# A single ring of up-projected expert inputs, 30 tiles deep, in a fused pooling/retention/PEER block on one core

## Chip, core and metric

One NeuronCore of a Trainium2 chip runs the whole block in one launch. The metric is device time in microseconds (us); three runs of the kernel before took 1885.77, 1891.47 and 1893.0, median 1891.47. The profiled execution is another run of the same kernel.

## What is computed

The input is 512 latent tokens and 256 context tokens of width 1024, all in float32. A first half (adaptive norm, pooling mixer, bidirectional retention, gated merge) ends in a residual x. The change lies in the second half, a product-key expert layer with 128 x 128 = 16384 single-neuron experts:

```python
q = (hb @ wq).reshape(t, 8, 2, 128)
s = einsum('thpd,hpkd->thpk', q, keys)
s1, i1 = top_k(s[:, :, 0], 16); s2, i2 = top_k(s[:, :, 1], 16)
cand = s1[..., :, None] + s2[..., None, :]      # 16 x 16 pairs per head
best, pos = top_k(cand, 16)                     # 16 experts per token and head
g = softmax(best)
act = gelu(einsum('thkd,td->thk', u[eidx], hb))
y = einsum('thk,thkd->td', g * act, v[eidx])
```

Then x + g2 * y goes through a final RMSNorm.

## The kernel before

Matrix products are made in three parts (`mm3`, lines 155 to 157): each float32 operand is split into a rounded high part (`hi`, a cast on ScalarE, line 167) and a low part (`lo = raw - hi`, line 172, on VectorE or GpSimd), and hi*hi, lo*hi and hi*lo are added up in PSUM. Weight tiles arrive as 128 x 1024 float32 (512 KB) in a ring of NRAW = 3 raw buffers, all by DMAs on SP's queue; hi and lo have four buffers each.

Of the 512 tokens the last 384 (NB = 3 blocks of 128) are computed *densely*: all 16384 experts are evaluated, and a matrix G of routing weights (zero where an expert was not chosen) masks them. The first block of 128 tokens is *gathered*: its 128 chosen experts per token are fetched one at a time by indirect DMA (a fetch is 128 rows of u and v, 1 MB).

The expert part runs under a manual schedule: each engine executes in the order in which the program issues, and a wait holds up all that is behind it on the same engine or DMA queue. Its stages:

1. **Queries** (`heads`, 735 to 862). For eight heads: load and split `wq`, project, score against the keys, and run the top-k of the dense blocks (`topk`, a generator: `next` advances it by one step: best 16 of each half, pair sums and index sums on GpSimd, best 16 of 54 pairs with one-hots `oh`, product `oe`, reduction to expert numbers `ef`). Between them run the first *ups*.
2. **An up** (`up_steps`, 1068): for expert column tile j, 24 matmuls give hT x u[j] (128 experts x 384 tokens) in PSUM, and a Gelu on ScalarE writes tile `a` of 384 columns (line 1077). `ups` (864) makes the first AHEAD = 24 of them ahead of the loop; `run_up(n)` advances it by n halves of an up. The tiles lie in `a0`, a block of 22 that shares a pool with the first block's top-k, and in a ring of NA = 3.
3. **Routes** (994): softmax, expert numbers split into two 7-bit halves, everything turned by transposes and copied wide to fp16 (`i12`, `gq`).
4. **One-hots and weights** (1023 to 1056, loop at 1140): in 24 steps of 16 tokens VectorE makes one-hots (`eq`, `o1`, two products `o2`), TensorE multiplies them into the block of G, ScalarE evicts it (`st`) and writes it to DRAM (`gd`); half an up runs in each step.
5. **The dense loop** (1166 to 1220), 128 rounds. Round j adds `a[j]*G[j]` times v[j] into six PSUM banks Y (`down`, 18 matmuls), makes `ph` and `pl` for round j+1, splits v for the next round, splits u and runs the up of tile j + LA (so the first 21 rounds have none, and the lead of 24 is used up by them down to LA = 3). G is read back in 16 pages of 8 tiles (`place`, 1086). In rounds below VU = 19 v is split by GpSimd, else by VectorE. `tick` (1129) advances the first block's top-k, a new head every second round. From round GATHER = 21 on, 1.5 experts per round (CREDIT) are fetched, multiplied (`dot`, 960) and added (`combine`, 969), both on VectorE, two rounds after they were asked for. NUV = 6 fetch buffers are taken from the space that `a0` and the top-k leave.
6. **The tail** (1221 on): the last Y matmuls, final norm and output.

Of the kernel before, what the change touches and what calls it, by code (L numbers as in the profile page):

```python
# [39 lines left out]
AHEAD = 24  # L40
NA = 3
A0 = AHEAD - NA + 1
LA = 3
VU = 19
END = 125
LATE = 114
GATHER = 21
LAG = 2
CREDIT = 1.5
# [89 lines left out]
class Build:  # L139
# [67 lines left out]
    def build(self):  # L207
        nc, tc, I = self.nc, self.tc, self.I
        with ExitStack() as es:
            dr = es.enter_context(tc.tile_pool(name="dram", bufs=1, space=bass.MemoryType.DRAM))  # L210
# [482 lines left out]
    def peer(self):  # L693
# [6 lines left out]
        self.ioh = mr.tile([P, P], F16, name="ioh")  # L700
        self.early = ExitStack()
        self.queries()

    def queries(self):
        nc, tc, I = self.nc, self.tc, self.I
        hT = self.hT
        with tc.tile_pool(name="out", bufs=1) as p:
# [7 lines left out]
        self.a0 = self.early.enter_context(tc.tile_pool(name="a0", bufs=1, side="right")).tile(  # L715
            [P, A0, NB * P], F32, name="a0")
# [6 lines left out]
        self.iota = tp.tile([P, P], F32, name="iota")  # L723
        nc.sync.dma_start(self.iota, I["kc"][:, K_IOTA:K_IOTA + P])
        nc.gpsimd.tensor_copy(self.ioh, self.iota)
        s0 = tp.tile([P, PH, 1, 2, P], F32, name="s0")
        self.acts, self.us = [], {}
        with tc.manual_schedule():
            self.heads(kp, s0, h0)
            es.close()  # L730
            self.topk0 = [self.topk(tp, h, s0[:, h], [0], 4) for h in range(PH)]
            self.z0 = tp.tile([P, PH], F32, name="z0")
            self.experts()

    def heads(self, kp, s0, h0):
# [44 lines left out]
        def u_load(n):  # L780
            if n < QU:
                uraw[n] = self.rt.tile([P, 4 * N], F32, name="ur", tag="i12", bufs=1)[:, :D]
                nc.sync.dma_start(uraw[n], I["uvd"][n, :, :D])

        def u_split(n):
            hi, lo = [kp.tile([P, D], F32R, name=x, tag=x, bufs=1) for x in ("uhi", "ulo")]
            nc.scalar.copy(hi, uraw[n])
            nc.vector.tensor_tensor(lo, uraw.pop(n), hi.bitcast(F32), ALU.subtract)
            self.us[n] = hi, lo

        uraw = {}
# [5 lines left out]
        for h in range(PH + 1):  # L797
            load(h + 2)
            if h % 2 == 0:
                u_load(h // 2)  # L800
            if h < PH:
                split_hi(h + 1)
                q = [query(h, 0)]
                if h + 1 < PH:
                    ws[h + 1] = [self.split_lo(raws[h + 1][0], ws[h + 1][0], nc.gpsimd), ws[h + 1][1]]
            if h:
                next(steps[h - 1])
            if h < PH:
                q.append(query(h, 1))
            else:  # L810
                self.run_up(2)
# [5 lines left out]
            if h % 2 == 1 and h < PH:  # L817
                u_split(h // 2)
            if h:
                next(steps[h - 1])  # L820
            if h + 1 < PH:
                ws[h + 1] = self.columns([ws[h + 1][0], self.split_lo(raws[h + 1][1], ws[h + 1][1], nc.gpsimd)])
            if h == PH - 1:
                for n in range(QU, QU + 2):
                    self.us[n] = self.split_w(self.load_u(n), nc.gpsimd)
            if h:
                next(steps[h - 1])
                if h == PH - 1:
                    self.us[QU + 2] = self.split_w(self.load_u(QU + 2), nc.gpsimd)
                next(steps[h - 1])  # L830
            if h == PH:
                break
            s = kp.tile([P, NB, 2, P], F32, name="s", tag="s", bufs=2)
            steps[h] = self.topk(kp, h, s, list(range(1, TB)), 2, nc.vector if h == PH - 1 else None)
# [21 lines left out]
        self.run_up(5)  # L856
        for _ in steps.pop(PH - 1):
            pass
        z = kp.tile([P, NB * PH], F32, name="z")
        self.softmax(self.gw, z)  # L860
        self.run_up(6)
        self.routes(kp)

    def ups(self):

        for j in range(AHEAD):
            if QU <= j < AHEAD - 3:
                self.us[j + 3] = self.load_u(j + 3)
# [375 lines left out]
```

## Time and profile before

| | |
|---|---|
| runs, median of three | 1891.47 us |
| profiled execution, time and span | 1889.54 us, 1887.7 us |
| mean granted TensorE clock | 0.973 of full |
| PE (TensorE matmul) busy | 1752.4 us, 93% |
| PEld (its weight loads) busy | 1570.0 us, 83% |
| DVE (VectorE) busy | 1376.5 us, 73% |
| ACT (ScalarE) busy | 778.2 us, 41% |
| POOL (GpSimd) busy | 521.3 us, 28% |
| DMA | 404.00 MB, mean 214 GB/s |
| issue to landing, median: a load of u or v, 512 KB | 6.3 us |
| issue to landing, median: a page of G, 1536 KB | 15.0 us |

Busy time counts an engine's instructions on one execution of the program; a matmul that waits in the array or runs at the lower of the clock's two levels (1.2 and 2.4 GHz) counts with its whole duration, and neighbouring matmuls overlap. Times within the span are counted from its first instruction. A releaser in square brackets is what ended the idle time before an instruction.

### The profile page before, as it was taken

How to read it: one execution, taken by the hardware profiler on the slowest of the kernel's cores; microseconds unless marked ns; L12 is line 12 of the kernel's file. 1: busy time of each engine (PE TensorE's matmuls, PEld its weight loads, DVE VectorE, ACT ScalarE, POOL GpSimd, SP SyncE). 2: the span in 40 equal slices, each digit the busy share in tenths (PEclk: the TensorE clock that was granted, in tenths of full speed). 3: DMA queues.
4: the chain of work that ended last, by engine and by line, in shares of the span. 5: the costliest groups of instructions: out<-in, count | busy, mean ns of one | idle time of the engine just before them, and what ended most of it. 6: DMA issues, size and time to landing. Idle time of an engine off the chain costs nothing.

```text
span 1887.7 us, 25975 instructions
## 1 busy us (share of the span) xinstructions
PE 1752.4 (93%) x9913; PEld 1570.0 (83%) x9913; DVE 1376.5 (73%) x2374; ACT 778.2 (41%) x1321; POOL 521.3 (28%) x414
## 2 busy tenths in 40 slices
PE   7999999999999877758798999999999999999997
PEld 4889988888999877756577998899999999989996
DVE  6865455663669989948876787788878888876445
ACT  6343234232433257742233443344444444444332
POOL 2222120010347732217652222223223223320000
PEclk9999999999999989988899999999999999999998
DMA  7211144772332236554348988889998998986442
GB/s 302 96 46 45 62 134 155 235 262 85 112 114 90 68 105 236 229 212 140 107 163 314 345 324 305 326 320 343 336 344 323 360 347 324 346 316 198 142 160 89
DMA packets 132380, 404.00 MB, mean 214 GB/s; under 512 B 9632, under 2 KB 59040, under 8 KB 112672
## 3 DMA queue, kind: packets, MB, share of 16 engines
q1 hardware_dynamic: 109936, 241.38, 37.5%
q0 software_dynamic: 18432, 134.23, 18.2%
q10 hardware_dynamic: 3888, 26.74, 3.4%
q8 instruction: 77, 1.26, 0.3%
q14 instruction: 47, 0.39, 0.1%
HBM read 372.95 MB, written 29.36 MB: 213 GB/s over the span
## 4 chain that ended last, share of the span: by engine, by line
PE 71%; DVE 16%; DMA 4%; ACT 2%; issue 2%; POOL 1%; SPq 0%; DVEq 0%; ACTq 0%; POOLq 0%
PE ps L157 16%; PE ps L155 16%; PE ps L156 16%; PE Y L156 7%; PE Y L157 7%; PE Y L155 7%; DVE o L1042 4%; DMA raw<-uvd 4%; DVE eq L1039 2%; DVE o L1040 1%; DVE pl L150 1%; DVE a L1110 1%; ACT hi L167 1%; DVE pos L925 1%; POOL lo L172 1%
## 5 line engine op out<-in xcount | busy, mean ns | idle before, releaser
L167 ACT CAST hi<-raw 128x1024 fp32r<-128x1024 f32 x332 | 343.7, 1050 | 288.8 <-DMA raw<-uvd 205.9
L172 DVE TENSOR_TENSOR lo<-raw,hi 128x1024 fp32r<-128x1024 f32 x258 | 319.1, 1237 | 121.7 <-ACT hi L167 120.2
L155 PE MATMUL ps<-hfT,hi 128*128 128x384 f32 x1120 | 381.3, 340 | 4.6 <-ACT a L1077 4.6
L157 PE MATMUL ps<-hfT,lo 128*128 128x384 f32 x1120 | 377.9, 337 | 1.1 <-DVE lo L172 1.1
L156 PE MATMUL ps<-hfT,hi 128*128 128x384 f32 x1120 | 377.3, 337 | 0.2 <-POOL hfT L150 0.2
L955 POOL DMA_INDIRECT uv<-uv,eidx x128 | 207.2, 1619 | 523.5 <-DVE acc L974 474.8
L155 PE MATMUL Y<-hi,ph 128*128 128x512 f32 x768 | 307.0, 400 | 48.2 <-ACT ph L149 37.9
L156 PE MATMUL Y<-lo,ph 128*128 128x512 f32 x768 | 307.7, 401 | 4.0 <-DVE lo L172 2.5
L157 PE MATMUL Y<-hi,pl 128*128 128x512 f32 x768 | 307.3, 400 | 0.9 <-DVE pl L150 0.9
L172 POOL TENSOR_TENSOR lo<-raw,hi 128x1024 fp32r<-128x1024 f32 x74 | 194.4, 2634 | 356.9 <-ACT hi L167 355.7
L155 PEld LDWEIGHTS ps<-hfT,hi 128*128 128x128 f32 x1120 | 212.6, 190 | 9.0 <-ACT a L1077 5.0
L156 PEld LDWEIGHTS ps<-hfT,hi 128*128 128x128 f32 x1120 | 212.4, 190 | 4.7 <-POOL hfT L150 0.6
L155 PEld LDWEIGHTS Y<-hi,ph 128*128 128x128 f32 x768 | 148.2, 193 | 81.2 <-ACT ph L149 41.6
L157 PEld LDWEIGHTS ps<-hfT,lo 128*128 128x128 f32 x1120 | 211.8, 189 | 2.0 <-DVE lo L172 2.0
L150 DVE TENSOR_TENSOR pl<-a,ph 128x384 fp32r<-128x384 f32 x128 | 90.8, 710 | 137.4 <-ACT ph L149 137.3
L156 PEld LDWEIGHTS Y<-lo,ph 128*128 128x128 f32 x768 | 148.0, 193 | 35.5 <-DVE lo L172 4.0
L157 PEld LDWEIGHTS Y<-hi,pl 128*128 128x128 f32 x768 | 147.9, 193 | 34.5 <-DVE pl L150 3.1
L974 DVE SCALAR_TENSOR_TENSOR acc<-uv,act,acc 128x1024 f32<-128x1024 f32 x127 | 163.0, 1283 | 18.5 <-ACT act L966 8.7
L1077 ACT ACTIVATE a<-ps 128x384 f32<-128x384 f32 x128 | 62.6, 490 | 276.2 <-PE ps L157 271.7
L963 DVE SCALAR_TENSOR_TENSOR uv<-uv,hf 128x1024 f32<-128x1024 f32 x128 | 152.9, 1219 | 0.0
L1055 ACT ACTIVATE st<-ps 128x512 f32<-128x512 f32 x96 | 90.5, 1104 | 25.5 <-PE ps L1054 24.9
L1110 DVE TENSOR_TENSOR a<-a,G 128x384 f32<-128x384 f32 x128 | 86.1, 674 | 19.2 <-DMA G<-gd 19.2
(282 smaller groups left out, 2911.6 us busy)
## 6 DMA issues: line engine op xcount, KB each, us to landing
raw<-uvd SPq DMA_DIRECT2D x252, 512.0 KB, 6.3
ada<-ada SPq DMA_DIRECT2D x48, 512.0 KB, 4.8
gd<-st ACTq DMA_DIRECT2D x24, 1024.0 KB, 4.4
G<-gd SPq DMA_DIRECT2D x16, 1536.0 KB, 15.0
raw<-w_in SPq DMA_DIRECT2D x44, 512.0 KB, 4.1
raw<-wq SPq DMA_DIRECT2D x16, 512.0 KB, 3.9
raw<-ret_out SPq DMA_DIRECT2D x8, 512.0 KB, 5.0
raw<-w_out SPq DMA_DIRECT2D x8, 512.0 KB, 3.7
```

The lines of the kernel that those rows point to most:

```text
L150: (eng_lo or nc.vector).tensor_tensor(lo, src, hi.bitcast(F32), ALU.subtract)
L155: mm(out, a[0], b[0], start=first, stop=False)
L156: mm(out, a[0], b[1], start=False, stop=False)
L157: mm(out, a[1], b[0], start=False, stop=last)
L167: self.nc.scalar.copy(hi, raw)
L172: eng.tensor_tensor(lo, raw, hi.bitcast(F32), ALU.subtract)
L955: self.nc.gpsimd.indirect_dma_start(out=t, out_offset=None, in_=self.I["uv"], in_offset=bass.IndirectOffsetOnAxis(ap=self.eidx[:, s:s + 1] ...
L963: nc.vector.scalar_tensor_tensor(t[:, :D], t[:, :D], 1.0, self.hf, ALU.mult, ALU.mult, accum_out=act[:, 0:1])
L974: nc.vector.scalar_tensor_tensor(self.acc, t[:, D:], act[:, 1:2], self.acc, ALU.mult, ALU.add)
L1042: nc.vector.tensor_tensor(wide(o2[:, r]), wide(eq), tokens(self.gq[:, r]), ALU.mult)
L1055: nc.scalar.mul(st[:, :, t:t + 4].rearrange("p m t -> p t m"), ps, 1.0 / GSCALE)
L1110: nc.vector.tensor_tensor(a, a, Gs[j // MG][:, :, j % MG], ALU.mult)
```

## The change

- The lead grows from AHEAD = 24 to 30 up tiles. They lie in one ring of 31 buffers in a pool of its own, so the first block's top-k leaves its space early and the gather starts at GATHER = 8 with CREDIT = 1.2 instead of at 21 with 1.5. LATE moves from 114 to 117, and the tail's tiles take three of the fetch buffers.
- In the loop `goal(j)` says how many ups are done after round j: 30 + (j + 1) * 98 // 121. So about four rounds in five have an up, from round 1 to round 120, and the lead shrinks evenly.
- v is split by GpSimd in rounds 0 to 7 only. The first block's top-k gets a new head in every tick, five ticks run ahead of the loop, and its buffers are halved (`oh` and `oe` have one).
- The first page of G is read in four pieces: two while one-hot steps are still running (after steps 13 and 20), two after the last; v 0 and 1 are asked for ahead of those two. Page 0 and all even pages lie in a pool of their own.
- In the one-hot stage every third step runs two halves of an up; low parts of u are made by VectorE there (`prep`), by GpSimd during the last head only.
- The end of the query stage is put in another order: Exp on ScalarE before the last product, softmax before the last reduction, the gate weights turned first, two index copies on two engines, ups between them.

In the loop over the heads the ninth pass (top-k steps and ups after the last head) is dissolved into the lines after the loop, and `prep` takes the place of three splits of u. The diff, without that loop, the constants that the text names and the allocations that move with them:

```diff
-        self.run_up(5)
-        for _ in steps.pop(PH - 1):
+
+        last = steps[PH - 1]
+        self.run_up(2)
+        self.prep(QU + 2, nc.gpsimd)
+        next(last)
+        next(last)
+        for _ in steps.pop(PH - 2):
             pass
+        self.prep(QU + 3, nc.gpsimd)
+        next(last)
+        self.run_up(3)
+        next(last)
+        nc.scalar.activation(self.gw, self.gw, AF.Exp)
+        next(last)
+        self.run_up(4)
+        self.prep(QU + 4, nc.vector)
         z = kp.tile([P, NB * PH], F32, name="z")
-        self.softmax(self.gw, z)
-        self.run_up(6)
+        self.softmax(self.gw, z, False)
+        for _ in last:
+            pass
         self.routes(kp)
+    def ask(self, to):
+
+        for n in range(self.ul, min(to, AHEAD)):
+            self.uraw[n] = self.load_u(n)
+            self.ul = n + 1
+
+    def prep(self, n, eng):
+        if n < AHEAD and n not in self.us:
+            self.ask(n + 3)
+            self.us[n] = self.split_w(self.uraw.pop(n), eng)
+
     def ups(self):
         for j in range(AHEAD):
-            if QU <= j < AHEAD - 3:
-                self.us[j + 3] = self.load_u(j + 3)
-            if QU + 2 < j + 2 < AHEAD:
-                self.us[j + 2] = self.split_w(self.us[j + 2], self.nc.gpsimd)
+            if j > QU + 2:
+                self.prep(j + 1, self.nc.vector)
...
-        oh = tp.tile([P, n * 16, NC], F16, name="oh", tag="oh", bufs=1 if b0 else 2)
+        oh = tp.tile([P, n * 16, NC], F16, name="oh", tag="oh", bufs=1)
...
-        oe = tp.tile([P, n, 16, NCAND], F32, name="oe", tag="oe", bufs=1 if b0 else 2)
+        oe = tp.tile([P, n, 16, NCAND], F32, name="oe", tag="oe", bufs=1) if not b0 else \
+            self.rt.tile([P, 2 * NB * P * NI], F32, name="oe", tag="ig", bufs=1)[:, :n * 16 * NCAND].rearrange(
+                "p (n k c) -> p n k c", n=n, k=16)
...
-        self.i12 = dp.tile([P, 2, N, NI], F16, name="i12", tag="i12", bufs=1)
-        self.gq = dp.tile([P, 2, N, NI], F16, name="gq")
+        ig = dp.tile([P, 4, N, NI], F16, name="ig", tag="ig", bufs=1)
+        self.i12, self.gq = ig[:, 0:2], ig[:, 2:4]
         rep = [P, N, NI]
         ei = rp.tile([P, N], I32, name="ei", tag="qq", bufs=2)
         et = rp.tile([P, N], I32, name="et", tag="qq", bufs=2)
         ij = rp.tile([P, 2, N], F32, name="ij", tag="s", bufs=2)
         gT = rp.tile([P, 2, N], F32, name="gT", tag="s", bufs=2)[:, 0]
+
+        def turned(src):
+            pt = self.ps()
+            for b in range(NB):
+                nc.tensor.transpose(pt[:, b * P:(b + 1) * P], src[:, b], self.ident)
+            return pt[:, :N]
+
+        nc.scalar.mul(gT, turned(self.gw), GSCALE)
+        gT = gT.unsqueeze(2).to_broadcast(rep)
+        nc.scalar.copy(self.gq[:, 0], gT)
         nc.vector.tensor_copy(ei, self.ef.rearrange("p b k -> p (b k)"))
         nc.vector.tensor_scalar(et, ei, 7, None, ALU.logical_shift_right)
         nc.vector.tensor_scalar(ei, ei, 127, None, ALU.bitwise_and)
+        nc.vector.tensor_copy(ij[:, 1], ei)
         nc.vector.tensor_copy(ij[:, 0], et)
-        nc.vector.tensor_copy(ij[:, 1], ei)
-        for q in range(3):
-            pt = self.ps()
-            for b in range(NB):
-                src = ij[:, q, b * P:(b + 1) * P] if q < 2 else self.gw[:, b]
-                nc.tensor.transpose(pt[:, b * P:(b + 1) * P], src, self.ident)
-            if q < 2:
-                nc.scalar.copy(self.i12[:, q], pt[:, :N].unsqueeze(2).to_broadcast(rep))
-            else:
-                nc.scalar.mul(gT, pt[:, :N], GSCALE)
-        gT = gT.unsqueeze(2).to_broadcast(rep)
-        nc.scalar.copy(self.gq[:, 0], gT)
+        self.run_up(3)
+        ij = ij.rearrange("p q (b k) -> p q b k", b=NB)
+        i2 = turned(ij[:, 1])
+        i1 = turned(ij[:, 0])
+        nc.scalar.copy(self.i12[:, 0], i1.unsqueeze(2).to_broadcast(rep))
         nc.vector.tensor_tensor(self.gq[:, 1], gT, self.gq[:, 0], ALU.subtract)
+        nc.vector.tensor_copy(self.i12[:, 1], i2.unsqueeze(2).to_broadcast(rep))
...
-        a = self.a0[:, j] if j < A0 else mr.tile([P, N], F32, name="a", tag="a", bufs=NA)
+        a = self.ring.tile([P, N], F32, name="a", tag="a", bufs=AHEAD + 1)
...
-            Gs[p] = dp.tile([P, N // NT, MG, NT], F32, name="G", tag="G", bufs=NG)
-            nc.sync.dma_start(Gs[p], self.gd[:, :, p * MG:(p + 1) * MG])
+            Gs[p] = (dp if p % 2 else self.g0).tile([P, N // NT, MG, NT], F32, name="G", tag="G", bufs=1)
+
+        def read(p, b0=0, b1=N // NT):
+            nc.sync.dma_start(Gs[p][:, b0:b1], self.gd[:, b0:b1, p * MG:(p + 1) * MG])
...
+            place(0)
             for i, t0 in enumerate(todo):
                 for n in range(len(oh), min(i + NH, len(todo))):
                     oh[n] = self.onehots(todo[n], hp)
-                self.run_up(1)
+                self.run_up(2 if i % 3 == 2 else 1)
                 self.weights(t0, oh[i], hp)
+                if i in (13, 20):
+                    read(0, *{13: (0, 10), 20: (10, 18)}[i])
         self.rt_es.close()
-        self.dp = dp = es.enter_context(tc.tile_pool(name="dense", bufs=1))
-        place(0)
+        for n in range(2):
+            vs[n] = load_v(n)
+        nv[1] = 2
+        read(0, 18, 22)
+        read(0, 22)
+        self.dp = dp = self.pool("dense")
+        place(1)
+        read(1)
+        for _ in range(5):
+            self.run_up(1)
+            tick()
         self.run_up(2 * AHEAD)
-        place(1)
         run_v(1, nc.gpsimd)
         self.pes.close()
         self.pp = es.enter_context(tc.tile_pool(name="pd", bufs=1, space=PSUM))
...
         S = PH * TOPK
         slots, fetched, done, credit = {}, 0, 0, 0.0
         asked = [0] * LAG
-        nu = AHEAD
-        ns = nl = nu
+        nu = ns = nl = AHEAD
+
+        def goal(j):
+
+            return min(P, AHEAD + (j + 1) * (P - AHEAD) // JE)
+
         acts.update(enumerate(self.acts))
         run_times(3)
         ps[0] = weigh(0, nc.vector)
...
                 self.acc = self.gp.tile([P, D], F32, name="acc", bufs=1)
             if j % MG == MG - 2 and j // MG + 2 < P // MG:
                 place(j // MG + 2)
-            deep = j < VU or j >= END
+                read(j // MG + 2)
+            deep = j >= JE
             if j + 1 < P:
                 ps[j + 1] = weigh(j + 1, nc.vector)
-            run_v(min(P, max(j + 2, min(j + 4, VU)) if j < END else j + 4), nc.gpsimd if j < VU else nc.vector)
-            while nl < min(P, j + LA + 3) and nl < nu + 3:
+            run_v(min(P, j + 4 if deep else j + 2), nc.gpsimd if j < GATHER else nc.vector)
+            while nl < goal(j + 2):
                 us[nl] = self.load_u(nl)
                 nl += 1
             hi = {}
-            for n in range(ns, min(nl, j + LA + 2)):
+            for n in range(ns, goal(j + 1)):
                 hi[n] = self.split_hi(us[n])
             if j < P - 2:
                 for b in range(NB):
...
             ready = list(range(done, asked[0]))
             cr = [self.dot(s, slots[s]) for s in ready]
-            run_times(j + (4 if deep else 3))
+            run_times(j + 4)
             for s, act in zip(ready, cr):
                 self.combine(s, slots.pop(s), act)
             done = asked[0]
             for n in hi:
                 us[n] = self.split_lo(us[n], hi[n], nc.vector)
                 ns += 1
-            while nu < min(ns, j + LA + 1):
+            while nu < goal(j):
                 acts[nu] = self.up(nu, us.pop(nu))
                 nu += 1
-            tick(j % 2 == 0)
+            tick()
             if j == GATHER - 1:
                 self.softmax(self.gw0, self.z0)
             if j >= GATHER:
...
                     credit -= 1
             asked = asked[1:] + [fetched]
             if j == LATE:
-                fin = [self.gp.tile([P, D], F32, name=f"fin{i}", bufs=1) for i in range(6)]
+                assert fetched == S
+                fin = [self.gp.tile([P, 2 * D], F32, name="uv", tag="uv", bufs=NUV) for _ in range(3)]
+                fin = [x[:, i * D:(i + 1) * D] for x in fin for i in range(2)]
                 self.row_bcast(fin[0], self.modc[:, 24:32])
                 nc.sync.dma_start(fin[1], I["fg"].to_broadcast([P, D]))
```

## Rows read from the trace of the kernel before

**Rows 1.** Busy us (x instructions) of each engine, granted clock, DMA share, GB/s, by stretch.

```profile
643.00:684.06 41.06, 32.52 (x177) 31.84 (x175) 31.77 (x89) 17.22 (x23) 22.91 (x18) 0.90 0.28 90
684.06:822.20 138.14, 102.94 (x1014) 95.50 (x1015) 137.29 (x96) 103.48 (x115) 37.84 (x12) 0.92 0.54 206
...
848.30:979.00 130.70, 104.61 (x394) 81.28 (x395) 116.40 (x283) 37.60 (x64) 82.58 (x109) 0.89 0.37 116
979.00:1250.00 271.00, 258.50 (x1279) 232.83 (x1278) 202.23 (x250) 107.91 (x208) 74.64 (x49) 0.97 0.87 323
1250.00:1680.00 430.00, 429.98 (x2174) 391.01 (x2173) 355.30 (x437) 184.10 (x360) 127.38 (x78) 1.00 0.91 339
```

**Rows 2.** PE's timeline in the loop: start, us, line, operation.

```profile
1401.15 0.39 PE L155 MATMUL Y<-hi,ph 128*128 128x512 f32 x1
...
1405.27 0.33 PE L155 MATMUL ps<-hfT,hi 128*128 128x384 f32 x1
...
1409.45 0.39 PE L155 MATMUL Y<-hi,ph 128*128 128x512 f32 x1
```

**Rows 3.** The same on PE and DVE, between the one-hots and the first round.

```profile
833.75 0.34 PE L157 MATMUL ps<-hfT,lo 128*128 128x384 f32 x1
...
841.30 1.50 DVE L1110 TENSOR_TENSOR a<-a,G 128x384 f32<-128x384 f32 x3 [19.16 <-DMA G<-gd]
...
848.30 0.79 PE L155 MATMUL Y<-hi,ph 128*128 128x512 f32 x1 [14.21 <-ACT ph L149]
```

**Rows 4.** DVE's timeline, from the routes to the first one-hot.

```profile
682.20 1.76 DVE L1021 TENSOR_TENSOR gq<-gT,gq 128x1536 f16<-128x1536 f32 x1 [7.84 <-ACT gq L1020]
...
684.06 3.17 DVE L1039 TENSOR_TENSOR eq<-ioh,i 128x2048 f16<-128x2048 f16 x1
```

**Rows 5.** DVE's timeline in the one-hot steps: pairs of products.

```profile
697.62 2.36 DVE L1042 TENSOR_TENSOR o<-eq,gq 128x2048 f16<-128x2048 f16 x2
...
702.29 4.55 DVE L1042 TENSOR_TENSOR o<-eq,gq 128x2048 f16<-128x2048 f16 x2
```

**Rows 6.** DVE by line from 1250 to 1680 us: busy us, mean ns, idle before.

```profile
L172 DVE TENSOR_TENSOR lo<-raw,hi 128x1024 fp32r<-128x1024 f32 x103 | 125.8, 1221 | 36.5 <-ACT hi L167 36.2
L974 DVE SCALAR_TENSOR_TENSOR acc<-uv,act,acc 128x1024 f32<-128x1024 f32 x77 | 98.8, 1284 | 11.8 <-ACT act L966 6.0
L963 DVE SCALAR_TENSOR_TENSOR uv<-uv,hf 128x1024 f32<-128x1024 f32 x77 | 91.9, 1219 | 0.0
```

**Rows 7.** DVE's timeline in the early rounds: the first block's top-k.

```profile
904.24 1.04 DVE L940 TENSOR_REDUCE e<-oe 128x16 f32<-128x864 f32 x1
...
911.02 0.28 DVE L898 FIND_INDEX8 si<-sv,s 128x8 uint32<-128x128 f32 x1
```

**Rows 8.** Timeline of two early rounds, PE, POOL and DVE.

```profile
898.36 0.56 DVE L150 TENSOR_TENSOR pl<-a,ph 128x384 fp32r<-128x384 f32 x1 [0.68 <-ACT ph L149]
...
898.38 0.50 PE L155 MATMUL Y<-hi,ph 128*128 128x512 f32 x1 [2.40 <-ACT ph L149]
...
899.35 2.41 POOL L172 TENSOR_TENSOR lo<-raw,hi 128x1024 fp32r<-128x1024 f32 x1 [4.82 <-ACT hi L167]
...
899.72 2.45 DVE L150 TENSOR_TENSOR pl<-a,ph 128x384 fp32r<-128x384 f32 x1 [0.34 <-ACT ph L149]
...
912.00 0.80 PE L155 MATMUL Y<-hi,ph 128*128 128x512 f32 x1 [5.03 <-ACT ph L149]
...
913.02 0.63 PE L157 MATMUL Y<-hi,pl 128*128 128x512 f32 x1
...
913.45 0.63 PE L155 MATMUL Y<-hi,ph 128*128 128x512 f32 x1
```

**Rows 9.** The chain of waits at the gather's start: start, us, what.

```profile
980.36 24.65 DMA raw<-uvd
```

**Rows 10.** PE's waits from 1000 to 1250 us: total, times, longest.

```profile
PE Y L155 <- ACT hi L167: 10.3, 3, 5.6
```

**Rows 11.** PE's timeline at the end: the last matmul.

```profile
1874.47 0.39 PE L157 MATMUL Y<-hi,pl 128*128 128x512 f32 x1
```

More of the change, by code (lines that the diff above doesn't have):

```diff
@@ L39 @@
 NH = 2
[L40 to L47, printed above, removed]
+AHEAD = 30
+JE = 121
+LATE = 117
+GATHER = 8
 LAG = 2
-CREDIT = 1.5
+CREDIT = 1.2
 NT = 16
@@ L714, in queries @@
         self.xs.close()
-        self.a0 = self.early.enter_context(tc.tile_pool(name="a0", bufs=1, side="right")).tile(
-            [P, A0, NB * P], F32, name="a0")
+        self.ring = self.pool("ring", side="right")
         tp = self.early.enter_context(tc.tile_pool(name="topk0", bufs=1, side="right"))
@@ L730, in queries @@
             es.close()
-            self.topk0 = [self.topk(tp, h, s0[:, h], [0], 4) for h in range(PH)]
+            self.topk0 = [self.topk(tp, h, s0[:, h], [0], 2) for h in range(PH)]
             self.z0 = tp.tile([P, PH], F32, name="z0")
@@ L796, in heads @@
         self.ahead = self.ups()
-        for h in range(PH + 1):
+        for h in range(PH):
             load(h + 2)
+            if h == PH - 2:
+                self.ask(QU + 2)
             if h % 2 == 0:
                 u_load(h // 2)
-            if h < PH:
+            last = h == PH - 1
+            if not last:
                 split_hi(h + 1)
-                q = [query(h, 0)]
-                if h + 1 < PH:
-                    ws[h + 1] = [self.split_lo(raws[h + 1][0], ws[h + 1][0], nc.gpsimd), ws[h + 1][1]]
+            q = [query(h, 0)]
+            if last:
+                self.prep(QU, nc.gpsimd)
+            else:
+                ws[h + 1][0] = self.split_lo(raws[h + 1][0], ws[h + 1][0], nc.gpsimd)
             if h:
                 next(steps[h - 1])
-            if h < PH:
-                q.append(query(h, 1))
-            else:
-                self.run_up(2)
+            q.append(query(h, 1))
             if h:
@@ L816, in heads @@
                     pass
-            if h % 2 == 1 and h < PH:
+            if h % 2 == 1:
                 u_split(h // 2)
+            if last:
+                self.prep(QU + 1, nc.gpsimd)
+            else:
+                ws[h + 1] = self.columns([ws[h + 1][0], self.split_lo(raws[h + 1][1], ws[h + 1][1], nc.gpsimd)])
             if h:
                 next(steps[h - 1])
[L821 to L826, printed above, removed]
                 next(steps[h - 1])
-                if h == PH - 1:
-                    self.us[QU + 2] = self.split_w(self.load_u(QU + 2), nc.gpsimd)
                 next(steps[h - 1])
-            if h == PH:
-                break
             s = kp.tile([P, NB, 2, P], F32, name="s", tag="s", bufs=2)
-            steps[h] = self.topk(kp, h, s, list(range(1, TB)), 2, nc.vector if h == PH - 1 else None)
+            steps[h] = self.topk(kp, h, s, list(range(1, TB)), 2, nc.vector if last else None)
             scores(h, 0, q[0], s)
```

31 lines of the change are left out of this document (18 added, 13 removed).

## The prediction

> **What bounds the kernel now.** I read the page's slices first: TensorE (PE) is busy nearly everywhere except in a stretch from about 640 to 1000 us. Busy time is no measure of matmul work there (a matmul that runs at the lower clock is longer), so I cut the span at the marks of the expert stage and read the busy time and granted clock of each piece [rows 1]. From 1250 to 1680 us PE is busy 429.98 of 430.00 us at clock 1.00: it alone sets the pace. The PE timeline of one round there [rows 2] gives the prices of the work: 18 matmuls into Y take 4.12 us (1401.15 to 1405.27), one input tile "up" (24 matmuls into ps) 4.18 us (1405.27 to 1409.45), so a round costs 8.30 and 52 rounds fill the 430 us.
>
> With these prices the loop of 128 rounds needs 128 x 4.12 + 104 x 4.18 = 962 us. It runs from the first Y matmul (848.30) to the end of the tail's matmuls (about 1875) [rows 3, 11]: 1027 us, 65 more than PE needs. Rounds 0 to 20 hold no up (24 lie ready), so 21 rounds need 86.5 us of PE and take 130.7 [rows 1]: 44 lost. Another 20 go between 979 and 1250, where the gather starts. Ahead of the loop, the one-hot stage is bound by VectorE (DVE), busy 137.29 of 138.14 us with PE at 102.94; then 14.21 us pass between the last up and the first Y matmul [rows 3]; and from 643 to 684 PE has 32.52 busy of 41.06.
>
> **The change, part by part.** The matmuls are the same ones; 6 of the 104 ups move ahead of the loop (lead 24 to 30) and the other 98 are spread over rounds 0 to 120. The gain can only be PE's idle time.
>
> *(a) End of the query stage: 10 us less.* Before, the exponent, the softmax and the three transposes follow one another, and DVE sits 7.84 us until ScalarE (ACT) has written gq; the first one-hot starts at 684.06 [rows 4]. Now the softmax comes ahead of the last index reduction, the gate weights are turned first, one of the four wide copies goes to DVE, and ups are put between. On PE 12 halves of an up (2.09 each, half of 4.18) stand behind 643, with the transposes some 27 us: to about 671. On DVE the 7.84 wait goes, and a wide copy of about 1.8 comes (the nearest row is gq, 1.76). PE's transposes come after the three last halves, so eq starts about 3 us behind them: 674. Bounds: 670 (PE alone) to 684 (the wait moves and does not go).
>
> *(b) One-hot stage: 4 us less.* Before, 24 halves run in it, so 12 weight splits by GpSimd (POOL). The pair of one-hot products takes 2.36 us alone and 4.55 where a POOL split lies beside it [rows 5]: 12 x 2.19 = 26.3 us. Now 32 halves run (one more in every third step), and 16 splits are DVE's own at 1.22 [rows 6]: 19.5. 138.1 - 26.3 + 19.5 = 131.3. PE goes from 102.94 to 102.94 + 8 x 2.09 = 119.7 busy and ACT from 103.48 by four tiles more (about 6) to 110, so all three are close and will wait for each other now and then: I take 134. Bounds: 129 to 150 (a step pays each wait between the engines once more, 0.7 us x 24). The two early reads of G stand on SP's queue among the loads of u; they ask for blocks written several steps before, so I charge nothing.
>
> *(c) From the last one-hot product (822.20) to the first Y matmul (848.30): 26.1 becomes 30, 4 more.* Before, the reads of G leave after the last write, the loads of v behind them, and DVE waits 19.16 us for G [rows 3]. Now 18 of 24 blocks are already read, v 0 and 1 are asked for first (v 1 needs the raw buffer of u 27, whose split is late by a few us; the rest of G and the load of u 29 queue behind it). But this stretch now also holds 9 halves of an up (18.8 us of PE, 4 before) and five steps of the first block's top-k on DVE. A head costs DVE 7.06 us from its reduction to the last index of the next head's first step [rows 7], first and last of 27 rows; the five steps hold about 3.4 heads, 24 us, and three splits 3.7. With products and split of the first tile (2.5) that is 30. Bounds: 22 (PE's halves alone) to 38 (u 29 behind the second G page: the last write lands some 10 after, then by the table's medians 15.0 for a page and 6.3 for a load, split and up 6.4).
>
> *(d) The loop: 1027 becomes 971, 56 less.* Rounds 0 to 7: about 32 us of top-k remain for DVE, most in rounds 0 to 2. Each such round has a head (7), pl and the product (1.1), a u split (0.81 x 1.22), some 2 us in which a POOL split of v holds DVE up (pl 2.45 beside the split of 2.41, 0.56 without [rows 8]) and 1 us of waits for ACT: 12 us in each of three rounds. Rounds 3 and 4 have 9.5, rounds 5 to 7 are PE's at 7.5. Sum 77, where PE needs 58. Bounds: 62 to 105.
> Rounds 8 to 120: 113 x 4.12 + 92 x 4.18 = 850. Is PE still the bound? DVE was busy 355.3 us in 52 rounds, 6.83 each, 83% of 8.27 [rows 1]. A round now has 1.81 splits for 2 and 1.2 gathered experts for 1.48 (77 in 52): with 1.22 for a split and 1.284 + 1.219 an expert, that is 0.9 less: 5.9 of 7.52 (850/113), 79%. DMA: v and 0.81 u of 0.52 MB, 1.2 experts of 1.05 MB and 0.2 MB of G make 2.4 MB in 7.52 us, 319 GB/s, where 339 had no stall [rows 1]. ACT and POOL are freer than before. So PE stays the bound.
> Rounds 121 to 127: 7 x 4.12 = 29. When the gather starts POOL asks for six experts at once; before, a load of u or v then took 24.65 us and PE waited 10.3 in all for such weights [rows 9, 10], with the lower clock after it about 20 in that stretch. Demand is lower now but the burst is the same: 15. Sum 77 + 850 + 29 + 15 = 971. The new wait that takes the place of the old is DVE in rounds 0 to 2.
>
> A wait in every step would cost PE the clock too, and the rows say when: after an idle of 2.40 us the next matmuls follow at full spacing, after one of 5.03 us they run at half clock, 0.43 instead of 0.23 apart [rows 8]. The Trainium skill, TensorE: Matmul & The Clock Gate, section "HAM oscillation — how this bites in real kernels", speaks against this loop: a PE that is starved once in every step of a loop pays a throttled start each time. By it, each of the 21 rounds without an up after round 7 would end in such a start, 13 matmuls 0.2 us later as after the gap of 5.03: 21 x 2.6 = 55, 1880 in all. By the rows a gap of 1 to 2 us there costs only itself, and the sum stays.
>
> *Sum.* 10 + 4 - 4 + 56 = 66 less; the end after the last matmul (13 us) stays. The profiled execution has span 1887.7 and took 1889.54, 0.1% under the median of 1891.47: 1889.5 - 66 = 1823.5. With the median's 2 us: **1825**.
>
> **The rivals.**
> *Rounds without an up starve PE, mildly.* In 21 of rounds 8 to 120 PE has only 4.12 us of work, DVE and ACT, each in program order, 5 to 7. For it: rounds 0 to 20 took 6.2 each in just this shape. Against: pl and the split of v for round j+1 stand first in DVE's round j, so DVE has most of a round in hand. At 1.5 us each 31 more, 1856. Chance 0.14.
> *The first rounds stay bound.* If the one buffer for oh and oe makes POOL and DVE take turns, rounds 0 to 7 cost 13 each, 104 for 77: 1852. Chance 0.10.
> *The reads in pieces don't do what they say.* If a read of blocks 0 to 9 holds up the next write of the same DRAM tensor, ACT's queue (writes and evictions) stands twice for some 8 us: 1841. Chance 0.08.
> *Slower.* The same up-less rounds, but with two experts due in one of them: DVE then has 6 + 2.6 + 1 = 9.6 us against 4.12, 5.5 too many, and at a gap that long the clock falls as in rows 8 (13 matmuls 0.2 later, 2.6). At 21 x 5.5 = 116 the time is 1941, at the clock's price as well near 1990. It decides from 66/21 = 3.1 us a round. Against: one round in five has two experts, and the two cycles meet only about every fifth time. Chance 0.06; half-way cases that come out near the time before (gaps just long enough to drop the clock in each of the 21 rounds, 55 more) 0.04.
>
> **How the numbers follow.** Forecast 0.58 at 1825 (its own range 1805 to 1845), rivals 0.14, 0.10, 0.08, 0.06 and 0.04. Everything below 1860 but the last two and the worse half of the first is inside 1802 to 1862; below 1802 (all lower bounds of a to c and rounds 0 to 7 at 62) I leave 0.06. A measurement tells 0.5% (9 us) from no change: faster 0.90, same 0.04, slower 0.06.
>
> **What would show it.** Right: first one-hot at about 674, last 134 later, first Y matmul near 838, rounds 0 to 2 at 12 us with PE waiting for ph or lo, from then on PE busy without gaps and clock 1.00, Y and ps matmuls still 4.12 and 4.18 a group, last Y near 1809. Wrong: idle PE in each round without an up, DVE over 95% busy after round 8, loads of u or v over 15 us past the gather's start, or a stage ahead of the loop that grew by the ups it took in.

## The result, and the profile after

The changed kernel took 1837.15 us (median of four runs, 1836.28 to 1851.27) against 1890.37 for the kernel before: ratio 0.9741, 95% interval 0.9698 to 0.9785. The forecast was 1825 (1802 to 1862).

The profiled execution is the longest of the four, with a span of 1849.3. The busy times of the whole span: TensorE (PE) holds the same work as before in a span that is 38 us shorter, VectorE (DVE) is far from full.

```profile
PE 1751.0 (95%) x9913; PEld 1566.5 (85%) x9913; DVE 1346.7 (73%) x2402; ACT 776.6 (42%) x1320; POOL 435.6 (24%) x387
```

Its windows by stage, to be laid beside [rows 1] (same columns): end of the queries, one-hots, the gap to the first Y matmul, first rounds, loop.

```profile
643.00:673.71 30.71, 27.91 (x161) 26.70 (x159) 29.04 (x89) 14.39 (x19) 11.52 (x13) 1.00 0.26 88
673.71:800.68 126.97, 111.41 (x1098) 104.35 (x1097) 125.86 (x111) 104.46 (x119) 0.00 (x0) 0.97 0.67 244
800.68:843.50 42.82, 29.55 (x152) 26.64 (x152) 26.87 (x124) 16.34 (x30) 10.69 (x42) 0.84 0.52 174
843.50:912.00 68.50, 60.04 (x267) 50.51 (x268) 58.27 (x140) 21.23 (x36) 40.87 (x55) 0.95 0.40 131
...
1250.00:1680.00 430.00, 416.96 (x2034) 371.95 (x2033) 322.02 (x399) 170.93 (x325) 99.43 (x66) 0.98 0.83 305
```

Two things to see. The gap (its window, of 42.82 us, ends 0.5 us ahead of the first Y matmul) has PE busy for 29.55 at clock 0.84. And from 1250 to 1680, where PE had no gap before [rows 1], 13 us are idle now, at a *lower* DMA share (0.83 for 0.91).

**The gap.** PE's timeline, where an up (a product of hT with an input tile) waits twice for the cast hi of its tile, and the matmuls behind each wait last 0.52 to 0.69 (half clock) instead of 0.33; then ScalarE's (ACT) timeline, where that cast stands behind the top-k's copies sf, which wait for DVE:

```profile
821.29 0.69 PE L151 MATMUL ps<-hfT,hi 128*128 128x384 f32 x1 [4.08 <-ACT hi L163]
...
834.57 0.69 PE L151 MATMUL ps<-hfT,hi 128*128 128x384 f32 x1 [5.98 <-ACT hi L163]
...
844.00 0.50 PE L151 MATMUL Y<-hi,ph 128*128 128x512 f32 x1 [1.92 <-ACT ph L145]
```

```profile
833.19 0.22 ACT L927 ACTIVATE sf<-si 128x16 f32<-128x16 uint32 x1 [5.33 <-DVE si L919]
833.37 0.20 ACT L928 CAST sf<-si 128x16 f32<-128x16 uint32 x1
833.48 1.04 ACT L163 CAST hi<-raw 128x1024 fp32r<-128x1024 f32 x1
```

**The stalls in the loop.** Behind the first three rounds, those of 10 to 16 us are numbered 24, 40, 56, 64, 72, 76, 88, 96 and 104 (the length of number k is the time from the pl of tile k on DVE to the next; pl is made a round ahead of PE): all but one multiples of 8, just behind the rounds (j % 8 = 6) in which SP issues the read of a whole page of G, 1.5 MB. One of them on SP's queue, in the chain of waits (start, us, what) and on PE:

```profile
1325.96 0.53 SPq L1120 DMA_DIRECT2D G<-gd  x1
1327.37 12.75 SPq L158 DMA_DIRECT2D raw<-uvd  x1
```

```profile
1327.37 20.38 DMA raw<-uvd
1347.77 1.05 ACT hi L163
```

```profile
1344.55 0.39 PE L153 MATMUL Y<-hi,pl 128*128 128x512 f32 x1
1348.87 0.65 PE L151 MATMUL Y<-hi,ph 128*128 128x512 f32 x1 [3.93 <-ACT hi L163]
...
1350.72 0.63 PE L153 MATMUL Y<-hi,pl 128*128 128x512 f32 x1
1351.15 0.63 PE L151 MATMUL Y<-hi,ph 128*128 128x512 f32 x1
```

A weight load asked for 1.4 us after this page of G lands 20.38 us later (the profile's list of DMA issues has 5.8 as the median of all 252 loads of u and v); PE idles 3.93 us, and then runs at half clock (0.43 apart, before 0.23). The second line shows where most of that time goes: on SP's queue the issue of this load alone takes 12.75 us, where an issue takes 0.33 at the median, and the next two loads are asked for right behind its end, at 1340.2 and 1340.7. Behind the other pages of the loop it takes 2 to 11 us.

### The profile page after: what moved, and what is told of

Same layout as the page of the kernel before. It is cut to its first block, busy times and chain, and to the rows that moved or that the text cites. A ratio compares the mean times of both kernels' runs of the same rounds, so it can differ in the third digit from the quotient of the medians.

```text
span 1849.3 us, 25951 instructions
## 1 busy us (share of the span) xinstructions
PE 1751.0 (95%) x9913; PEld 1566.5 (85%) x9913; DVE 1346.7 (73%) x2402; ACT 776.6 (42%) x1320; POOL 435.6 (24%) x387
## 4 chain that ended last, share of the span: by engine, by line
PE 38%; DVE 9%; DMA 8%; ACT 4%; issue 3%; POOL 1%; ACTq 0%; DVEq 0%; POOLq 0%
DMA raw<-uvd 8%; PE Y L152 7%; PE Y L153 7%; PE Y L151 7%; PE ps L153 6%; PE ps L151 6%; PE ps L152 6%; DVE lo L168 2%; DVE o L1071 2%; ACT st L1084 2%; ACT hi L163 2%; DVE eq L1068 1%; DVE uv L987 1%; DMA gd<-st 1%; DVE o L1069 0%
## 5 line engine op out<-in xcount | busy, mean ns | idle before, releaser
L168 DVE TENSOR_TENSOR lo<-raw,hi 128x1024 fp32r<-128x1024 f32 x285 | 358.6, 1259 | 139.8 <-ACT hi L163 138.4
L979 POOL DMA_INDIRECT uv<-uv,eidx x128 | 196.5, 1535 | 623.7 <-DVE acc L998 599.2
L151 PE MATMUL Y<-hi,ph 128*128 128x512 f32 x768 | 305.4, 398 | 16.5 <-ACT hi L163 12.8
L168 POOL TENSOR_TENSOR lo<-raw,hi 128x1024 fp32r<-128x1024 f32 x47 | 117.8, 2515 | 204.5 <-ACT hi L163 204.5
L146 DVE TENSOR_TENSOR pl<-a,ph 128x384 fp32r<-128x384 f32 x128 | 75.0, 586 | 118.5 <-ACT ph L145 118.5
L1084 ACT ACTIVATE st<-ps 128x512 f32<-128x512 f32 x96 | 90.9, 1111 | 13.4 <-DMA gd<-st 7.2
L989 ACT ACTIVATE act<-act 128x1 f32<-128x1 f32 x128 | 25.9, 202 | 162.4 <-DVE uv L987 162.2
## 6 DMA issues: line engine op xcount, KB each, us to landing
G<-gd SPq DMA_DIRECT2D x15, 1536.0 KB, 14.3
```

Source lines behind the costliest of these rows:

```text
L146: (eng_lo or nc.vector).tensor_tensor(lo, src, hi.bitcast(F32), ALU.subtract)
L151: mm(out, a[0], b[0], start=first, stop=False)
L168: eng.tensor_tensor(lo, raw, hi.bitcast(F32), ALU.subtract)
L979: self.nc.gpsimd.indirect_dma_start(out=t, out_offset=None, in_=self.I["uv"], in_offset=bass.IndirectOffsetOnAxis(ap=self.eidx[:, s:s + 1] ...
L1084: nc.scalar.mul(st[:, :, t:t + 4].rearrange("p m t -> p t m"), ps, 1.0 / GSCALE)
```

## The experiments

All are the changed kernel with one to three edits. Times are medians; each ratio is to the kernel before on the same chip. Four chips were used, so that small differences between kernels of different chips (of a few us) are read from the traces. Lengths of rounds are those between two starts of pl on DVE. The theory for the loop was P (the whole pages of G), its rival U (the rounds without an up).

**The changed kernel again**, no edit.

> The changed kernel again, nothing edited. All theories: 1837 us, 0.972 of the kernel before, runs up to 1851. It is the yardstick for the runs beside it.

1838.51 us, ratio 0.9706 (0.9676 to 0.9735). Its profile (span 1836.4) is the one to size terms with:

```profile
842.30:917.10 74.80, 66.76 (x302) 56.74 (x303) 60.92 (x145) 24.32 (x39) 41.70 (x55) 0.95 0.41 134
917.10:1786.00 868.90, 851.40 (x4209) 762.19 (x4208) 655.55 (x812) 353.74 (x666) 196.75 (x128) 0.99 0.83 304
```

The second line is 112 rounds, for which PE needs 112 x 4.12 + 91 x 4.18 = 842 us: 27 are lost. The long rounds are the same ones (13.8 at 24, 11.6 at 40, 11.5 at 56, 12.2 at 64, 12.4 at 72, 11.6 at 76, 13.4 at 88, 10.2 at 96, 14.4 at 104). In the profiled execution shown above the same rounds lost some 10 us more.

**Pages of G in pieces.**

```diff
-            if j % MG == MG - 2 and j // MG + 2 < P // MG:
-                place(j // MG + 2)
-                read(j // MG + 2)
+            p, i = divmod(j - 5, MG)
+            if j >= 5 and p + 2 < P // MG and i < 6:
+                if i == 0:
+                    place(p + 2)
+                read(p + 2, 4 * i, 4 * i + 4)
```

Each piece is 256 KB, and the first one goes out a round earlier than the whole page did.

> Pages of G after the second are read in six pieces of four blocks over six rounds instead of one read in one round. Theory P (a page's 1.5 MB in one burst holds the loads of u and v up; that is why every eighth round took 10 to 16 us in the profile): these rounds fall to about 8, PE's waits after round 8 (23 us with the clock lost after them some 30) go to under 8, 10 to 20 us less, 1820 to 1828. Rival U (what starves PE is the round without an up; that pages lie there is chance): the same long rounds, 1837 within 4.

1818.87 us, ratio 0.9596 (0.9569 to 0.9623): 19.6 less than without the edit. The long rounds are gone, and the same 112 rounds take 850.1, 8 us over PE's need, at clock 1.00. Of these 8, 4.8 are one round of 12.9, number 12, that has 8.1 with whole pages: now pieces of a page are read where the gather starts. No issue of a load on SP's queue takes over 1 us in this loop.

```profile
918.00:1780.00 862.00, 855.05 (x4267) 769.52 (x4266) 662.55 (x819) 358.31 (x671) 196.28 (x128) 1.00 0.85 308
```

P is shown, and U falls as a cause by itself: the rounds without an up are all still there (5.7 to 6.3 us) and starve nothing.

**A denser gather from round 21** (the lead's even use kept, and v still split by GpSimd in rounds below 8).

```diff
-GATHER = 8
-CREDIT = 1.2
+GATHER = 21
+CREDIT = 1.5
```

> The gather starts at round 21 with 1.5 experts a round, as before the change; ring of 30, even lead, the rest stay (GpSimd still splits v in rounds 0 to 7). Theory B (an even lead needs the gather spread out: 1.5 experts, 1.81 weights and G in 7.5 us are 2.7 MB, 365 GB/s, more than any stretch has moved): rounds 21 to 106 take 8.0 to 8.3 instead of 7.6, 35 to 60 us more, 1873 to 1898, nearly the whole gain. Rival S (the even lead does it alone, PE stays the bound): 1838 to 1848.

1892.92 us (ten runs, 1882.26 to 1902.18), ratio 0.9996 (0.9975 to 1.0018): the whole gain is gone, by the amount that B said. PE's waits for weights from the first Y matmul on (the changed kernel as first profiled: 12.8 in 5):

```profile
PE Y L151 <- ACT hi L163: 39.1, 9, 10.9
```

Rounds 24, 40, 48, 80 and 96 took 23.0, 15.6, 15.7, 14.5 and 15.4. This left open whether the denser gather fills the DMA engines, or makes the pages worse. **The same with the pages in pieces:**

> e4_late (the gather starts in round 21 instead of 8 and is denser; 1892.9 us) with the spread reads of G of e1_spread. Theory P (what the late gather loses, it loses where a whole page of G is read on top of it): the rounds of 23.0, 15.6, 15.7, 14.5 and 15.4 us at rounds 24, 40, 48, 80 and 96 fall to about 8.5, which is 42 us, so about 1850. Theory B (the denser gather alone fills the DMA engines; with 5 MB more in each 100 us there is no room whatever the order): the same bytes arrive as late in pieces, at least 1870.

1844.37 us, ratio 0.9735 (0.9703 to 0.9768), 48.6 less. Theory P: the 112 rounds went from 927 to 877.5 us, and these waits from 39.1 to 4.3. One long round is left, of 18.2 us, number 25, just behind one that P had fall to 8.5: it lies where the gather starts while a page is read, as number 12 in e1_spread, and there the pieces help little (24 and 25 together take 27.1 us, with whole pages 31.4). The other wait that is left is for DVE's part lo, on a DVE that splits and combines 1.5 experts a round (4.5 us in 4 waits in e1_spread's loop). PE's waits from the first Y matmul on:

```profile
PE ps L153 <- DVE lo L168: 16.3, 16, 1.3
PE Y L152 <- POOL lo L168: 6.5, 5, 1.9
PE Y L151 <- ACT hi L163: 4.3, 2, 3.8
```

So the early, thinner gather is worth 54.4 us with whole pages (1892.92 - 1838.51) and 25.5 with pieces (1844.37 - 1818.87).

**The old shape of the lead** (no up in rounds 0 to 26, then one in each), with the ring of 30 and the gather from round 8.

```diff
-            return min(P, AHEAD + (j + 1) * (P - AHEAD) // JE)
+            return min(P, max(AHEAD, j + 4))
-            run_times(j + 4)
+            run_times(j + (4 if j + 4 <= AHEAD or j >= 125 else 3))
```

> The lead shrinks in the old way: no up in rounds 0 to 26, then one in each round; ring of 30 and gather from round 8 stay. Theory S (the gain in the loop is the ups that now lie in the early rounds, which VectorE bounds anyway): rounds 8 to 26 have 4.1 us of PE against 5.5 of VectorE, 27 lost, rounds 27 to 124 take 8.3: 15 to 28 more, 1853 to 1866. Rival G (the early gather does it, the shape of the lead is worth nothing): 1838 within 5.

1857.27 us, ratio 0.9812 (0.9786 to 0.9838): with whole pages the even use is worth 18.8 us. What the old shape loses lies in the rounds without ups: behind the gather's start PE is busy 158.30 of 181.00 us at a DMA rate of 337 GB/s, and 12.5 of the 22.7 idle are one wait for a weight behind a whole page (round 16 took 20.2), so with pages in pieces the even use may be worth less; that was not run. From 1080 on next to nothing is lost, at 290 GB/s, though the pages are still read whole.

```profile
899.00:1080.00 181.00, 158.30 (x705) 131.42 (x704) 141.49 (x183) 68.31 (x136) 46.08 (x35) 0.94 0.89 337
1080.00:1780.00 700.00, 696.52 (x3525) 633.10 (x3524) 516.04 (x628) 286.17 (x533) 154.00 (x93) 1.00 0.80 290
```

**Low parts of u by GpSimd in the one-hot stage**, as before the change.

```diff
-                self.prep(j + 1, self.nc.vector)
+                self.prep(j + 1, self.nc.gpsimd)
```

> In the one-hot stage GpSimd makes the low parts of u again. Theory L (a split on GpSimd holds a product of VectorE up by 2.19 us where VectorE's own takes 1.22 or less): 16 splits cost about 15 us more, stage 127 to 142, 1853. Rival M (with 32 halves of an up in it the stage is PE's and ScalarE's as well, busy 111 and 104 of 127, and hides part): 5 us or less, 1838 to 1843.

1854.86 us (1851.86 to 1864.48), ratio 0.979 (0.9762 to 0.9818), 16.3 more: theory L. The pair of products takes 4.56 beside such a split, as in [rows 5]:

```profile
681.98 2.35 DVE L1071 TENSOR_TENSOR o<-eq,ig 128x2048 f16<-128x2048 f16 x2
...
686.65 4.56 DVE L1071 TENSOR_TENSOR o<-eq,ig 128x2048 f16<-128x2048 f16 x2
```

```profile
686.06 2.93 POOL L168 TENSOR_TENSOR lo<-raw,hi 128x1024 fp32r<-128x1024 f32 x1 [12.98 <-PE ps L1083]
```

The Trainium skill, SBUF — State Buffer, section "Who interferes with whom", says that VectorE and GpSimd share a port pair as an exclusive lock. The trace agrees: the pair started 0.6 us after the split of 2.93 us, which leaves 2.3 us, and took 2.2 us longer.

**The first page of G read whole**, after the last write (without the lines that read blocks 0 to 17 during the one-hots).

> The first page of G is read whole after the last one-hot step, as before the change; all else of the change stays. Theory A (the stretch is set by the top-k steps and the ups in it, the page is hidden): the page lands near 828 and is wanted at 836, 1837 within 4. Rival F (the pieces are what makes the stretch short): its 15 us come at the end of the writes, 8 to 12 more, 1845 to 1849.

1839.96 us (1838.78 to 1840.65) against 1838.51: at most 1.5. First Y matmul at 842.96 for 842.32. The page is hidden: it landed at 822.8, and DVE's first product with it, at 834.3, waited for nothing; the ups and the top-k steps beside it last longer.

**What makes the gap.** First, the splits of the last three tiles issued one top-k step earlier:

```diff
-        for _ in range(5):
+        for i in range(5):
             self.run_up(1)
+            if i % 2 == 0:
+                self.prep(27 + i // 2, nc.vector)
             tick()
```

> Ahead of the loop the splits of u 27, 28 and 29 are issued one half of an up earlier, before the top-k step instead of behind it. Theory A (ScalarE's queue: the cast hi of the next u stands behind the top-k's copies sf, which wait for VectorE; so PE stood 4.1 and 6.0 us): the stretch from the last one-hot product to the first Y matmul falls from 42.8 to about 34, 8 us less, 1829. Rival D (the load of u 29 is late, behind the page of G): PE waits as long, now for a cast that waits for a DMA and holds the copies up: 1837 to 1843.

1838.68 us, no change (1838.51). The first Y matmul came at 841.0 (842.3 in e0_same), and the waits for hi fell to 2.13 and 4.33 from 4.08 and 6.90: the cast had only moved behind the sf of the step before.

```profile
819.07 0.69 PE L151 MATMUL ps<-hfT,hi 128*128 128x384 f32 x1 [2.13 <-ACT hi L163]
...
831.26 0.69 PE L151 MATMUL ps<-hfT,hi 128*128 128x384 f32 x1 [4.33 <-ACT hi L163]
```

Then **no top-k steps ahead of the loop** (`tick()` out of that loop; GATHER = 12, CREDIT = 1.28, since the experts are known later; v is still split by GpSimd in rounds below 8):

> The five top-k steps of the first block ahead of the loop are taken out, so its top-k runs in rounds 0 to 11 and the gather starts at round 12 with 1.28 experts a round. Theory T (these steps, VectorE to ScalarE to GpSimd and back, set the stretch ahead of the loop, and PE in its gaps falls to the lower clock): the stretch falls from 42 to 25 or so, rounds 0 to 9 grow from 81 to about 96, 1838 within 6 in all. Rival C (the stretch is set by the load and the up of u 29): the stretch stays above 38 and the rounds still grow, 1850 or more.

1861.98 us, ratio 0.983 (0.9807 to 0.9854), 23.5 more. The gap fell by 8 to 35 us, with one wait of 6.00 for hi left (ACT's cast of the last tile waits there for its load, so the steps are one cause among two). The first eight rounds grew by as much (81.6 for 74.8), so that at round 9 this kernel is level (916.9 for 917.1): the steps cost the same in either place. The loss comes behind: the 112 rounds take 893.4 for 868.9, with 14.5, 11.6 and 15.1 at rounds 16, 24 and 32. That looks like the denser gather beside whole pages again, as in e4_late (with pieces this kernel was not run), and says nothing of the steps.

The next three start from the kernel with G in pieces (1818.87). **The copies sf by DVE**, where they need no wait for another engine (in the top-k of the gathered block, `b0` = 0):

```diff
-        nc.scalar.mul(sf[:, :, 0], si[:, :, 0], 128.0)
-        nc.scalar.copy(sf[:, :, 1], si[:, :, 1])
+        if b0:
+            nc.scalar.mul(sf[:, :, 0], si[:, :, 0], 128.0)
+            nc.scalar.copy(sf[:, :, 1], si[:, :, 1])
+        else:
+            nc.vector.tensor_scalar(sf[:, :, 0], si[:, :, 0], 128.0, None, ALU.mult)
+            nc.vector.tensor_copy(sf[:, :, 1], si[:, :, 1])
```

> e1_spread with one more edit: for the retrieval block the two short copies sf of a top-k step are made by VectorE, right behind the index search that they need, instead of by ScalarE. In e1_spread ScalarE waits 5.3 to 5.8 us for VectorE before sf in each step of 800 to 842 us, and 7.3 and 8.1 us in rounds 1 and 2; the cast hi of the next input tile and the gelu stand behind it. Theory A (that place in ScalarE's queue is what makes the gap after the one-hots 41.5 us long and rounds 0 to 2 15.1, 11.3 and 11.3 us): the gap falls to about 35, rounds 1 and 2 to about 8.3 each (4.1 of products and 4.2 of an up), the time from 1818.9 to about 1806. Rival B (the chain of VectorE and GpSimd through one step, or GpSimd's splits of 2.4 us, holds them): gap and rounds keep their lengths, 1819 within 3.

1812.85 us, ratio 0.9568 (0.9541 to 0.9594). Half of theory A: rounds 1 and 2 (from the pl of tile 2 on) fell from 11.3 to 9.4 and round 3 from 8.2 to 5.9, but the gap kept its 42 us (first Y matmul at 841.7 for 842.1). PE waits as long as before, 12.2 us from 800 to 845, now for the next part of the same tile, which stands behind a top-k step in DVE's queue:

```profile
PE ps L153 <- DVE lo L168: 11.7, 4, 6.4
```

**The second page of G read after the last up:**

> e1_spread with the second page of G (1.5 MB) read only after the last up ahead of the loop, instead of before the five top-k steps. In the kernels so far the last load of an input tile for the lead (asked at 820.3) lands behind that page, and TensorE waits 4 to 7 us before the last up. Theory U29 (the page holds that load): the gap after the one-hots falls from 41.5 us by 4 to 6, and the time to about 1814. Rival (the load isn't last; the cast behind the top-k copies is): gap 40 to 42, time 1819 within 2.

1820.72 us, ratio 0.9617 (0.9588 to 0.9646): theory U29 falls for this kernel; the first Y matmul came at 842.3, and PE waits 6.5 for the last hi (842.1 and 5.6 in e1_spread).

**sf by DVE and the splits one step earlier, together:**

> e9_sf and e2_preps together: the copies sf are on VectorE, and the splits of the last three input tiles of the lead are issued one top-k step earlier, ahead of that step's work on VectorE. In e9_sf TensorE waits 4.1 and 6.4 us in the gap, no longer for the cast hi but for the part lo, which stands behind a top-k step in VectorE's queue. Theory Q (the two queues hide one another: moving the cast alone or the copies alone can't free the up, both together can): these two waits go, the gap falls from 42 us to about 32, and the time from 1812.9 to about 1803. Rival (VectorE's own work of the steps, or the load of the last tile, is what lasts so long): gap 39 or more, and at least 1810.

1809.15 us (1808.66 to 1809.87), ratio 0.9562 (0.9537 to 0.9586), the lowest median of all. It ran on another chip than e9_sf, and the ratios (0.9562 and 0.9568) are no further apart than their intervals; what the edit does is read from the traces. The gap is 37.7 us (first Y matmul at 837.8 for 841.7), between theory and rival: PE's waits fell from 12.2 to 9.6 us, and the ups ran less of it at half clock (granted 0.91 in the gap for 0.88). What is left is in part a load, the last tile's, asked for behind the second page of G. PE's waits from 800 to 845, and ACT's cast:

```profile
PE ps L153 <- DVE lo L168: 5.8, 4, 2.6
PE ps L151 <- ACT hi L163: 3.8, 2, 3.7
```

```profile
825.09 1.04 ACT L163 CAST hi<-raw 128x1024 fp32r<-128x1024 f32 x1 [8.30 <-DMA raw<-uvd]
```

That this kernel would now gain by reading the page later was not tried.

## Why the prediction was right, step by step

Terms by the second profile of the changed kernel (e0_same); the sum of the steps was 66 less, measured 53 on the medians. That the time lay within the range is in part luck: one term was 7 us too cautious, and two were 12 and 11 too good. Two of the signs that I had named as wrong came: loads of over 15 us past the gather's start, and a stage ahead of the loop (the gap) that grew.

- **(a) Queries, -10: right.** First one-hot at 673.71 and 673.37, forecast 674. No run undoes a part of the new order, so which part gives the 10 us is not shown.
- **(b) One-hots, -4: too cautious by 7.** The stage took 127, not 134. Next to no wait between the engines was added by the ups (the 2.7 us that I had put on 131.3 for that), and the splits cost less than their 1.22: steps without one follow every 4.67 us, 24 x 4.67 = 112, which leaves 15 us for the 15 other instructions of DVE (111 less 4 in each step). These are the splits: 1.0 each, where I had 16 of 1.22. e7_pool shows the cause to be the right one.

```profile
673.71 1.23 DVE L1068 TENSOR_TENSOR eq<-ioh,ig 128x2048 f16<-128x2048 f16 x1
...
678.37 1.23 DVE L1068 TENSOR_TENSOR eq<-ioh,ig 128x2048 f16<-128x2048 f16 x1
...
683.04 1.23 DVE L1068 TENSOR_TENSOR eq<-ioh,ig 128x2048 f16<-128x2048 f16 x1
```

- **(c) The gap, +4: wrong, +16.** It took 42 to 43 against 30, past the upper bound of 38. I had added up DVE's work (24 of steps, 3.7 of splits) as if the other engines ran beside it. But a step goes DVE, ACT (sf), GpSimd and back, and an up goes ACT (hi), DVE (lo), PE: in queues that execute in order, each chain waits in the other's. Behind PE's waits of 4.1 and 6.9 the next products come at half clock. Freeing the cast alone (e2_preps) gained nothing, the copies alone (e9_sf) 6.0 us, 5.6 of it in the first rounds, both (e12_sf_preps) 9.7 (6.4 by the ratios), with the gap 4 shorter. So the two queues are shown for 4 of the 12 us; the rest lies in waits that e12_sf_preps still has (9.6 us, in part for a load), and no run takes them out.
- **(d) The loop, -56: -45, the sum nearly right, one term for a wrong reason.** Rounds 0 to 7: 74.8 for 77, with 15.2, 11.3 and 11.3 in the first three where I had 12 each. Part of what I charged to DVE there was the wait for sf (e9_sf: 69.0). For the 112 rounds behind: 868.9, where the forecast has 850 - 8.3 + 15 = 857. The 850 was right: PE's bare need is met within 8 us once the pages are spread. The 15 for stalls I had put at the start of the gather; there e0_same has no round over 9.6 (the start does cost where a page is read beside it: number 12 in e1_spread, 25 in e11_late_spread). The stalls were the pages of G, 19.6 us. They were in the trace of before as well, as SP's queue shows there (below): the load of 24.65 us in [rows 9] was asked for 1.6 us after a page, and its issue alone took 20.39; numbers 24, 40 and 48 took 17.6, 15.1 and 15.0 there. I read it as the gather's burst alone. I had counted G as 0.2 MB in each round, a mean; it comes as 1.5 MB in every eighth, on the queue of the weights. What stays open: from 1250 to 1680 the kernel before reads the same pages and PE loses nothing [rows 1]. There each round has an up, so that a tile of v is due every 8.30 us; with 98 ups in 121 rounds two are at times due 4.12 us apart. e5_old bears this out in part: with an up in every round and the same whole pages it loses 3.5 of 700 us from 1080 on. But the kernel before has an up in every round from 21 on too, and at 24, 40 and 48, with its denser gather, PE waited 5.6, 2.2 and 2.5 us. So the rounds without an up make the pages dearer and are not the whole of it; what else is stays open.

```profile
978.72 0.53 SPq L1089 DMA_DIRECT2D G<-gd  x1
980.36 20.39 SPq L162 DMA_DIRECT2D raw<-uvd  x1
```

**The rivals.** Mild starvation by the rounds without an up: not by themselves, by e1_spread; beside whole pages they may have a part in the 19.6 us. First rounds stay bound: no, 74.8 for the 104 it asked. Pieces that hold up the writes: no; its 1841 came near the time measured, but e6_whole without the pieces is no faster. Slower: no. The Trainium skill's rule (TensorE: Matmul & The Clock Gate, "HAM oscillation — how this bites in real kernels") asks for a wait in each step that is long enough; in these rounds there is none (PE waits 7 us in all from 918 to 1780 in e1_spread), the clock is 1.00 over these 862 us, and so its 55 us didn't come. Where a long wait did come, it cost the clock: after 3.93 us of idle the matmuls went 0.43 apart, as after 5.03 in [rows 8]. But the two lengths that I took from [rows 8] are no rule for gaps between them (last section).

## What to carry to other kernels

Count DMA load not as a mean over rounds but by what stands on the queue ahead of each weight tile: one page of 1.5 MB every eighth round cost 20 us here that the same bytes in six pieces don't. Where two chains cross several in-order engines, adding up the busiest engine's work is too low; write down, for each instruction that another engine waits for, what stands ahead of it in its own queue, and move both ends of the wait, since moving one may only show the other (the cast alone gained 0 us; with the copies moved first, the gap was 4 us shorter).

## What was not expected of the hardware

Weight loads of 512 KB, 5.8 us at the median, took 9 to 20 us (median 13.7) when asked for right behind a whole page of G in e0_same's loop, with the DMA engines at a mean share of 0.83: the mean says nothing of it. A good part of it is SP's queue itself, where the issue of that load takes 1.8 to 12.6 us for 0.33. In pieces of 256 KB a piece of G lands after 7.2 us, the whole page after 14.3 (both medians of the lists of DMA issues), and the rate over the loop is no lower with pieces (308 GB/s for 304).

The drop of the clock does not follow from the length of the one idle before it. In e5_old PE stood still for 2.25 us twice; after the first the matmuls go 0.23 apart, after the second 0.43, which is half clock:

```profile
894.62 0.50 PE L152 MATMUL Y<-lo,ph 128*128 128x512 f32 x1 [2.25 <-POOL lo L168]
...
895.20 0.40 PE L151 MATMUL Y<-hi,ph 128*128 128x512 f32 x1
895.43 0.40 PE L152 MATMUL Y<-lo,ph 128*128 128x512 f32 x1
...
1006.63 0.79 PE L152 MATMUL Y<-lo,ph 128*128 128x512 f32 x1 [2.25 <-DVE lo L168]
...
1007.65 0.63 PE L151 MATMUL Y<-hi,ph 128*128 128x512 f32 x1
1008.07 0.63 PE L152 MATMUL Y<-lo,ph 128*128 128x512 f32 x1
```

In e2_preps an idle of 2.13 us was followed by half clock too (shown above), and after 2.40 in [rows 8] the clock was full. What else decides, no run here tells.
